# Hybrid encoder trunk on one core: layer norm issued in two stages, the split of w_out spread over the attention, convolution taps and pacing shifted, and the first two chunks multiplied side by side

## Chip, core and metric

The kernel runs on one core of a Trainium2 chip. A run's time is the device time of that core in microseconds (us), and a time given for a kernel is the median over its runs. PE (TensorE) multiplies, DVE (VectorE), ACT (ScalarE) and POOL (GpSimd) do the elementwise work, and SP issues the transfers.

## What is computed

One encoder layer on two batches with shared weights, a prompt of 512 rows and a sample of 1024, model width 1024:

```python
h = _rmsnorm(x, norm_attn_g[l])
z = h @ w_in[l]                       # q, k, v, ca, cb
a_out = _window_attn(q, k, v, bias, band, attn_sink[l])
c = ca * jax.nn.sigmoid(cb)
c = _dwconv(c, conv_dw_w[l], conv_dw_b[l])          # 31 taps per channel
c = jax.nn.silu(_layernorm(c, conv_ln_g[l], conv_ln_b[l]))
x = x + jnp.concatenate([a_out, c], axis=-1) @ w_out[l]
h = _rmsnorm(x, norm_ffn_g[l])
u = _dwconv(h @ w_up[l], ffn_dw_w[l], ffn_dw_b[l])  # 3 taps
x = x + (jax.nn.silu(u[..., :D_FF]) * u[..., D_FF:]) @ w_down[l]
return _rmsnorm(x, norm_final_g)
```

## The kernel before, in words

All is float32. Each operand is split into a high part and the rest (hi, lo), and a product is three matmuls (hi hi, hi lo, lo hi): L296, L297 and L299 for the projections by w_in and w_up, L711 to L713 for the one by w_out. A weight chunk is 128 output columns of 8 blocks of 128 rows, so 24 matmuls. `split` makes hi with an ACT cast (L189) and lo with a POOL subtraction (L190).

The stages in order: RMS norm of the prompt's four row blocks and their transposes (L255, evacuated as hi by ACT L257 and lo by DVE L258); 14 chunks of w_in for the prompt and 14 for the two halves of the sample, each result evacuated on DVE (L369 and others); the prompt's out-projection; the prompt's up-projection, 22 chunks of two halves (evacuated by ACT L841 and DVE L837, with a three-tap convolution); the sample's out-projection; then a feed-forward part for the sample, and the final norm.

Beside these matmul loops go side items. `tick`, called between matmuls, lets each queue go on at a rate: `pace` holds them (RA, RB, RBO, RD, RN, RE for attention and norms; CA, CB, CL, CLO, CD for the convolution). The items are:

- the depthwise convolution of a channel block (`conv_items`): of 31 taps the last NOFF are offloaded, multiplied on ACT (L331) and added on POOL (L332); the others accumulate on DVE in a PSUM bank (L335 first, L339 after it);
- attention, in units: score matmuls (L560), sink column copies (L537) and exponents with row sums on DVE (L567), probability scaling (L589, L595), transposes (L616), value matmuls (L630, L631) and their evacuation by ACT L638 and L639, DVE L640 and POOL L642. Units 0 to 7 are the prompt's, 8 to 23 the sample's, two to a block of 128 rows;
- `conv_norm(i)`, layer norm and silu of block i: load from DRAM, four transposes (L675), mean and variance on DVE (L677, L678), the power on POOL (L173, L174), normalising on DVE (L681), a wait of YN = 2 steps, four transposes back (L687), ACT L690 to L694 and DVE L693 and L695. Blocks 0 to 3 are the prompt's;
- in the sample's attention, behind its last unit, loading and splitting w_out in 21 pieces of which each step does one.

A PSUM bank is one of eight, tags a (3), u (2), b (2) and c (1); `use` says which tags a job may take, and a job whose bank is not evacuated waits. Up to the sample's out-projection the program order so paced goes through a scheduler that interleaves the instructions of each engine; behind it the order is written out by hand. Each engine works through its own list in order, so an instruction that waits holds up all behind it.

Of the kernel before, what the change touches and what calls it, by code (L numbers as in the profile page):

```python
# [39 lines left out]
RA, RB, RBO, RD, RN, RE = 1.2, 0.8, 2.5, 0.8, 0.95, 0.9  # L40
# [3 lines left out]
CL, CLO, CD = 0.6, 1.0, 0.6  # L44

NOFF = (4, 7)
# [6 lines left out]
YN = 2  # L53
OB = "uc"
VG = 3
NW = 36
KEEP = 3
# [85 lines left out]
def tile_hybrid_encoder(ctx: ExitStack, tc: tile.TileContext, xs, rel_bias, norm_attn_g, w_in,  # L143
# [28 lines left out]
    def rstd_of(ss, n, out):  # L172
        nc.gpsimd.tensor_scalar(out, ss, 1.0 / n, EPS, op0=ALU.mult, op1=ALU.add)  # L173
        nc.gpsimd.tensor_tensor(out, out, nhalf[:], op=ALU.pow)  # L174
# [26 lines left out]
    raws, ws = {}, {}  # L201

    def want_raw(i):
        if i < nch and i not in raws and i not in ws:
            raws[i] = chunk_raw(w_in[0], order[i][2])

    def want_w(i):
        if i < nch and i not in ws:
# [28 lines left out]

    def norm_in_place(x, k):
# [8 lines left out]
        nc.vector.tensor_scalar_mul(x[:], x[:], rs[:])  # L247

    marks = []

    def transposed(xn, g, h):
        for kc in range(KC):
# [8 lines left out]
            marks.append((ia.ins, iv.ins))  # L261
# [30 lines left out]
    def proj(out, w, h, late_lo=False):  # L292
        whi, wlo = w
        for kc in range(KC):
# [3 lines left out]
            if not late_lo:  # L298
                nc.tensor.matmul(out, wlo[:, kc, :], hi[:], start=False, stop=(kc == KC - 1))  # L299
            if kc % 2 == 1 and kc < KC - 1:  # L300
                tick()
        for kc in range(KC if late_lo else 0):
            nc.tensor.matmul(out, wlo[:, kc, :], h[kc][0][:], start=False, stop=(kc == KC - 1))
# [11 lines left out]
    def conv_items(g, c, cp):  # L315
# [3 lines left out]
        noff = NOFF[g]  # L319
# [97 lines left out]
    def make_h1(nt):  # L417
        xt = xq.pop(nt)
        for k, x in enumerate(xt):
            if nt == 1:  # L420
                with tc.issue_after(marks[KC - 1][0]), tc.issue_after(marks[KC - 1][1]):
                    norm_in_place(x, k)
# [7 lines left out]
    def step(i, nt):  # L430
        kind, c, col = order[i]
        pp = bank("step")
        proj(pp[:], ws[i], h1[nt], i < 2 and nt == 0)
# [13 lines left out]
    with tc.issue_after(marks[KC - 1][0]):  # L447
        want_w(1)
# [39 lines left out]
    for i in range(npr):  # L488
# [5 lines left out]
        if i == 1:  # L494
            constants()
            bbd = bias_to_dram()
        want_raw(i + 2)
        want_w(i + 1)
        step(i, 0)
        ws.pop(i)  # L500
# [161 lines left out]

    def conv_norm(i):
        G, b = blocks[i]
        if G["g"] == 0:
            drain(convs)
        cat = cat_of(i, 1)
# [14 lines left out]
        del pt  # L682
        for _ in range(YN):
            yield 0.0
# [84 lines left out]

    def prompt():  # L770
        yield from attention(0, 8, {u: conv_norm(u - 4) for u in range(4, 8)})
# [128 lines left out]
    def sample():  # L900
        sink_columns()
        yield from attention(8, 24)
# [740 lines left out]
```

## Time and profile before

| quantity | value |
|---|---|
| median of three runs | 1564.2 us (1560.03 to 1566.33) |
| profiled execution | 1558.91 us, of which the span is 1557.1 |
| busy share of the span | PE 97%, DVE 72%, ACT 51%, POOL 46% |
| HBM | 164.74 MB read, 62.14 MB written, 146 GB/s over the span |

The first matmul of a projection starts at 17 us, the prompt's out-projection at 278, its up-projection at 376 (first lo product), the last up-projection ends at 682, the sample's out-projection follows to about 790. A timeline row has the start, the length, the engine, the line, the operation with out<-in, and in brackets the idle time before it with what ended it. A row of waits has what PE stood for, with the sum, the number of times and the longest.

### The profile page before, as it was taken

What the parts mean: (1) busy time and instruction counts of PE and PEld (TensorE: products, weight loads), DVE (VectorE), ACT (ScalarE), POOL (GpSimd) and SP (SyncE); (2) the same over time, 40 slices, a digit from 0 to 9 for tenths busy, and PEclk for the clock granted to TensorE, in tenths of its full rate; (3) what the DMA queues carried; (4) which work ended last, traced back from release to release, by engine and by line L of the source; (5) the groups of instructions that cost most, each with busy time, mean ns of one, the idle gap of its engine ahead of it and who ended that gap; (6) DMA issues with size and microseconds to landing.
All of it is one profiled execution on the core that took longest, in us unless ns stands there. A gap on an engine that the chain in (4) does not pass through costs nothing. (4 is left out here: it accounts for less than half of the span.)

```text
span 1557.1 us, 20112 instructions
## 1 busy us (share of the span) xinstructions
PE 1506.9 (97%) x6843; PEld 1229.4 (79%) x6843; DVE 1126.2 (72%) x1604; ACT 795.4 (51%) x1404; POOL 708.9 (46%) x566
## 2 busy tenths in 40 slices
PE   8899998999999999899999999999999999999997
PEld 6787787787888888777777888888888788888885
DVE  7999767857788785344868777777776845568883
ACT  4634654335787786633454444455545543444254
POOL 7652344226666776947433455555554000003355
PEclk9999999999999999999999999999999999999999
DMA  7582334447343346779332233333331582356644
GB/s 230 156 212 81 107 100 124 129 142 217 112 132 129 118 129 181 242 238 298 114 93 76 92 104 104 105 104 102 102 115 64 200 284 82 105 165 230 221 135 162
DMA packets 228780, 227.17 MB, mean 146 GB/s; under 512 B 13268, under 2 KB 168348, under 8 KB 228549
## 3 DMA queue, kind: packets, MB, share of 16 engines
q1 hardware_dynamic: 228677, 225.88, 45.8%
q8 instruction: 54, 0.88, 0.2%
q14 instruction: 49, 0.40, 0.1%
HBM read 164.74 MB, written 62.14 MB: 146 GB/s over the span
## 5 line engine op out<-in xcount | busy, mean ns | idle before, releaser
L190 POOL TENSOR_TENSOR q<-q,q 128x1024 fp32r<-128x1024 f32 x72 | 173.4, 2415 | 93.4 <-ACT q L189 34.4
L940 POOL TENSOR_TENSOR q<-q,q 128x512 fp32r<-128x512 f32 x101 | 140.0, 1391 | 164.0 <-ACT q L1050 151.7
L940 DVE TENSOR_TENSOR h<-h,h 128x512 fp32r<-128x512 f32 (+2 forms) x202 | 153.9, 794 | 65.2 <-ACT h L944 25.3
L1398 PE MATMUL w<-h,h 128*128 128x512 f32 x462 | 181.4, 393 | 1.4 <-DVE q L1185 1.4
L1399 PE MATMUL w<-h,h 128*128 128x512 f32 x462 | 181.5, 393 | 0.0
L1400 PE MATMUL w<-h,h 128*128 128x512 f32 x462 | 181.1, 392 | 0.0
L1064 PE MATMUL w<-h,q 128*128 128x512 f32 x448 | 176.5, 394 | 1.0 <-ACT h L1147 0.6
L1066 PE MATMUL w<-h,q 128*128 128x512 f32 x448 | 175.5, 392 | 1.0 <-POOL q L940 1.0
L1065 PE MATMUL w<-h,q 128*128 128x512 f32 x426 | 166.4, 391 | 0.0
L296 PE MATMUL u<-h,q 128*128 128x512 f32 x400 | 161.0, 403 | 5.4 <-DVE h L837 4.1
L297 PE MATMUL u<-h,q 128*128 128x512 f32 x400 | 158.6, 397 | 0.0
L299 PE MATMUL u<-h,q 128*128 128x512 f32 x384 | 151.8, 395 | 2.7 <-POOL q L190 2.7
L937 POOL TENSOR_TENSOR q<-q,q 128x1024 f32<-128x1024 f32 x12 | 32.4, 2707 | 236.6 <-DVE q L937 220.0
L339 DVE SCALAR_TENSOR_TENSOR c<-c,cvw,c 128x512 f32<-128x512 f32 x184 | 138.0, 750 | 2.9
L944 ACT CAST h<-h 128x512 fp32r<-128x512 f32 x120 | 71.9, 619 | 93.2 <-DVE h L940 41.9
L296 PE MATMUL b<-h,q 128*128 128x512 f32 x256 | 102.7, 401 | 3.3 <-DVE d L369 2.2
L1398 PEld LDWEIGHTS w<-h,h 128*128 128x128 f32 x462 | 86.8, 188 | 21.6 <-ACT h L944 1.8
L1400 PEld LDWEIGHTS w<-h,h 128*128 128x128 f32 x462 | 86.7, 188 | 19.7
L1399 PEld LDWEIGHTS w<-h,h 128*128 128x128 f32 x462 | 86.8, 188 | 19.5
L837 DVE SCALAR_TENSOR_TENSOR h<-u,fw,h 128x511 f32<-128x511 f32 x88 | 65.5, 744 | 49.8 <-ACT h L841 49.0
L299 PE MATMUL b<-h,q 128*128 128x512 f32 x256 | 101.4, 396 | 0.0
L297 PE MATMUL b<-h,q 128*128 128x512 f32 x256 | 101.1, 395 | 0.0
(417 smaller groups left out, 3670.4 us busy)
## 6 DMA issues: line engine op xcount, KB each, us to landing
q<-in_w_up SPq DMA_DIRECT2D x88, 512.0 KB
ga<-q SPq DMA_DIRECT2D x64, 256.0 KB
h<-ga SPq DMA_DIRECT2D x57, 256.0 KB
q<-in_w_in SPq DMA_DIRECT2D x28, 512.0 KB
h<-in_w_down SPq DMA_DIRECT2D x52, 256.0 KB
q<-in_x_sample SPq DMA_DIRECT2D x15, 512.0 KB
h<-qsd SPq DMA_DIRECT2D x24, 256.0 KB
x1d<-q SPq DMA_DIRECT2D x11, 512.0 KB
```

The costliest lines, as they stand in the source:

```text
L190: (nc.vector if dve else nc.gpsimd).tensor_tensor(lo[:], raw[:], hi[:].bitcast(F32), op=ALU.subtract)
L296: nc.tensor.matmul(out, whi[:, kc, :], hi[:], start=(kc == 0), stop=False)
L297: nc.tensor.matmul(out, whi[:, kc, :], lo[:], start=False, stop=False)
L299: nc.tensor.matmul(out, wlo[:, kc, :], hi[:], start=False, stop=(kc == KC - 1))
L339: nc.vector.scalar_tensor_tensor(acc[:], src(t), w(t), acc[:], op0=ALU.mult, op1=ALU.add)
L940: (eng or nc.vector).tensor_tensor(out, a, b, op=ALU.subtract)
L1064: nc.tensor.matmul(out, whi[:, s], hi[:], start=(start and c == 0), stop=False, **go)
L1065: nc.tensor.matmul(out, whi[:, s], lo[:], start=False, stop=False, **go)
L1066: nc.tensor.matmul(out, wlo[:, s], hi[:], start=False, stop=(stop and c == 3), **go)
L1398: nc.tensor.matmul(out, sh[:, c], th[:], start=(p == 0), stop=False)
L1399: nc.tensor.matmul(out, sh[:, c], tl[:], start=False, stop=False)
L1400: nc.tensor.matmul(out, sl[:, c], th[:], start=False, stop=(p == NPAIR - 1))
```

## The change

1. `conv_norm` is cut in two generators. `conv_norm_1` loads, transposes, and normalises; `conv_norm_2` transposes back and finishes. For the prompt, stage 1 of block u-3 comes behind unit u and stage 2 of it behind unit u+1, with stage 1 of the next; for the sample, stage 1 of blocks 4 and 5 comes first, and then stage 2 of one and stage 1 of the one two on.
2. The 21 pieces of w_out for the sample start behind unit WOU = 19, two at each unit, and what is left comes behind unit 23.
3. NOFF goes from 4 (prompt) and 7 (sample) to 7 for every prompt channel block, and 10, 10, 7, 7 for the sample's.
4. Rates: RD 0.8 to 0.84, RN 0.95 to 0.9, CL 0.6 to 0.45, CLO 1.0 to 0.8, CD 0.6 to 0.62.
5. `first_two` multiplies chunks 0 and 1 beside each other, block by block, in two banks. Their casts come ahead of the prompt's hi parts on ACT, and the transposes there may also take bank c. `late_lo` and the step order of these two chunks are dropped.
6. The RMS norm's odd row blocks take mean and epsilon in the DVE reduction, without POOL's multiply-add; the final norm takes the mean in ACT's square and has one POOL instruction fewer in `finish`.

```diff
-RA, RB, RBO, RD, RN, RE = 1.2, 0.8, 2.5, 0.8, 0.95, 0.9
+RA, RB, RBO, RD, RN, RE = 1.2, 0.8, 2.5, 0.84, 0.9, 0.9
-CL, CLO, CD = 0.6, 1.0, 0.6
-NOFF = (4, 7)
+CL, CLO, CD = 0.45, 0.8, 0.62
+NOFF = ((7, 7, 7, 7), (10, 10, 7, 7))
-YN = 2
+WOU = 19
...
     def norm_in_place(x, k):
...
-            nc.vector.tensor_tensor_reduce(out=junk[:], in0=x[:], in1=x[:], scale=1.0, scalar=0.0,
+            nc.vector.tensor_tensor_reduce(out=junk[:], in0=x[:], in1=x[:], scale=1.0 / D, scalar=EPS,
                                            op0=ALU.mult, op1=ALU.add, accum_out=ss[:])
-        rstd_of(ss[:], D, rs[:])
+        if k % 2 == 0:
+            root = rstd_of(ss[:], D, rs[:])
+        else:
+            root = nc.gpsimd.tensor_tensor(rs[:], ss[:], nhalf[:], op=ALU.pow)
...
-        noff = NOFF[g]
+        noff = NOFF[g][c]
...
+    def first_two():
+        pp = [bank("step") for _ in range(2)]
+        for kc in range(KC):
+            hi, lo = h1[0][kc]
+            for i in range(2):
+                whi = ws[i][0]
+                nc.tensor.matmul(pp[i][:], whi[:, kc, :], hi[:], start=(kc == 0), stop=False)
+                nc.tensor.matmul(pp[i][:], whi[:, kc, :], lo[:], start=False, stop=False)
+            if kc % 2 == 1:
+                tick()
+        for i in range(2):
+            for kc in range(KC):
+                nc.tensor.matmul(pp[i][:], ws[i][1][:, kc, :], h1[0][kc][0][:], start=False, stop=(kc == KC - 1))
+            kind, c, _ = order[i]
+            evac(kind, c, 0, pp[i][:])
...
-    for _ in make_h1(0):
+    use.update(turn="aubc")
+    for k, x in enumerate(xq[0]):
+        norm_in_place(x, k)
+    his = []
+    for i in range(2):
+        hi = sb.tile([KC, P], F32R)
+        nc.scalar.copy(hi[:], raws[i][:])
+        his.append(hi)
+    h1[0] = []
+    for _ in transposed(xq.pop(0), gA, h1[0]):
         pass
-    with tc.issue_after(marks[0][0]):
-        want_w(0)
+    use.update(turn="aub")
+    with tc.issue_after(marks[3]):
+        for i in range(2):
+            lo = sb.tile([KC, P], F32R)
+            nc.gpsimd.tensor_tensor(lo[:], raws.pop(i)[:], his[i][:].bitcast(F32), op=ALU.subtract)
+            ws[i] = his[i], lo
...
         nc.vector.tensor_scalar(xh[:], pt[:], mv[:, 0:1], rs[:], op0=ALU.subtract, op1=ALU.mult)
-        del pt
-        for _ in range(YN):
-            yield 0.0
+        normed[i] = xh
+        yield 0.0
+
+    def conv_norm_2(i):
+
+        cat, xh = cat_of(i, 1), normed.pop(i)
         p2 = bank("norm")
...
-        yield from attention(0, 8, {u: conv_norm(u - 4) for u in range(4, 8)})
+        yield from attention(0, 8, {u: both(*([conv_norm_2(u - 4)] if u > 3 else []), *([conv_norm_1(u - 3)] if u < 7 else []))
+                                    for u in range(3, 8)})
...
+        wos = wo_pieces()
+        yield from attention(8, 24, {u: some(wos, 2) for u in range(WOU, 24)})
         kt.clear(), vt.clear(), qt.clear(), bias.clear(), score_rows.clear()
         use.update(norm="a")
         pace.update(rate=RN)
+        yield from wos
         drain(late)
+        yield from conv_norm_1(4)
+        yield from conv_norm_1(5)
         for m in range(NE):
-            yield from conv_norm(4 + m)
+            yield from conv_norm_2(4 + m)
+            if NE + 4 + m < NB:
+                yield from conv_norm_1(4 + NE + m)
...
-            nc.scalar.activation(o[:, s], parts[n], AF.Square, accum_out=ss[:, n:n + 1])
-        nc.gpsimd.tensor_scalar(rs[:, 0:1], ss[:, 0:1], 1.0 / D, EPS, op0=ALU.mult, op1=ALU.add)
-        nc.gpsimd.tensor_scalar(rs[:, 1:2], ss[:, 1:2], 1.0 / D, rs[:, 0:1], op0=ALU.mult, op1=ALU.add)
+            nc.scalar.activation(o[:, s], parts[n], AF.Square, scale=D ** -0.5, accum_out=ss[:, n:n + 1])
+        nc.gpsimd.tensor_scalar(rs[:, 1:2], ss[:, 1:2], ss[:, 0:1], EPS, op0=ALU.add, op1=ALU.add)
```

How the order changes is shown at three places. Lines in the changed kernel have moved: L303 to L305 are the projection (L296, L297, L299 before), L600 the scores (L560), L607 the exponents (L567), L577 the sink copies (L537), L891 and L895 the up evacuation on DVE and ACT (L837, L841), L721 and L736 the norm's two transposes (L675, L687), L760 to L762 the out-projection (L711 to L713), L670 and L671 the values (L630, L631).

First, PE at the end of the prompt's attention, where the norm of the last blocks stands; before:

```order
L299 MATMUL b_149_2641<-h_105_649,q_383_2500 128x512
L675 MATMUL a_142_2510<-ident,q_370_2386 128x128 [waits DMAHW4_49,Activation_49]
L675 MATMUL a_142_2510<-ident,q_370_2386 128x128 x3
L687 MATMUL u_144_2540<-ident,q_387_2522 128x128 [waits DVE_49]
L687 MATMUL u_144_2540<-ident,q_387_2522 128x128 x3
L675 MATMUL a_150_2668<-ident,h_400_2660 128x128 [waits DMAHW6_49,PE_49]
L675 MATMUL a_150_2668<-ident,h_400_2660 128x128 x3
L687 MATMUL u_152_2701<-ident,h_404_2680 128x128 [waits DVE_49,Activation_49]
L687 MATMUL u_152_2701<-ident,h_404_2680 128x128 x3
L630 MATMUL a_148_2602<-h_391_2584,h_162_954 128x512 [waits Activation_49]
L711 MATMUL u_154_2812<-h_418_2765,h_216_1309 128x512 [waits Activation_49]
```

and now, where b_147, b_151 and b_153 are banks of w_in chunks for the sample:

```order
L303 MATMUL b_147_2618<-h_128_742,q_384_2405 128x512 [waits DVE_49]
L721 MATMUL a_145_2573<-ident,h_402_2564 128x128 [waits DMAHW5_49]
L721 MATMUL a_145_2573<-ident,h_402_2564 128x128 x3
L304 MATMUL b_147_2618<-h_129_743,q_384_2405 128x512
...
L304 MATMUL b_151_2696<-h_109_654,q_400_2553 128x512
L736 MATMUL u_150_2675<-ident,h_406_2585 128x128 [waits DVE_49]
L736 MATMUL u_150_2675<-ident,h_406_2585 128x128 x3
L305 MATMUL b_151_2696<-h_108_653,q_401_2554 128x512
L303 MATMUL b_153_2793<-h_128_742,q_400_2553 128x512 [waits DVE_49]
...
L305 MATMUL b_153_2793<-h_152_868,q_401_2554 128x512
L760 MATMUL u_152_2786<-h_429_2743,h_225_1329 128x512 [waits DVE_49,Activation_49]
```

Before, the first and second transposes of two blocks stood directly behind each other; now 54 rows of projections and attention stand between the two of the last block, and 25 matmuls behind them ahead of the out-projection.

Second, PE at the second block of the sample's attention, beside the prompt's up chunks (u_); before:

```order
L299 MATMUL u_180_3613<-h_503_3355,q_532_3557 128x512
L560 MATMUL b_187_3757<-q_507_3406,h_557_3732 128x256 [waits DVE_49]
L560 MATMUL b_187_3757<-q_508_3407,h_557_3732 128x256
L560 MATMUL a_192_3813<-q_509_3412,h_558_3734 128x256 [waits DMAHW6_49,DMAHW7_49,DMAHW2_49,DVE_49]
L560 MATMUL a_192_3813<-q_510_3413,h_558_3734 128x256 [waits DMAHW5_49]
L296 MATMUL u_181_3656<-h_487_3265,q_537_3601 128x512 [waits DVE_49,Activation_49]
L297 MATMUL u_181_3656<-h_488_3266,q_537_3601 128x512
```

and now four score pairs in a row, ahead of the next up chunk:

```order
L305 MATMUL u_181_3692<-h_516_3335,q_559_3638 128x512
L600 MATMUL b_187_3799<-q_528_3442,h_579_3771 128x256 [waits DVE_49]
L600 MATMUL b_187_3799<-q_529_3443,h_579_3771 128x256
L600 MATMUL a_192_3858<-q_530_3448,h_580_3773 128x256 [waits DVE_49]
L600 MATMUL a_192_3858<-q_531_3449,h_580_3773 128x256
L600 MATMUL a_199_3978<-q_528_3442,h_588_3823 128x384 [waits DMAHW6_49,DVE_49]
L600 MATMUL a_199_3978<-q_529_3443,h_588_3823 128x384
L600 MATMUL a_200_3982<-q_528_3442,h_588_3823 128x384 [waits DVE_49]
...
L303 MATMUL u_183_3745<-h_499_3241,q_565_3688 128x512 [waits DVE_49,Activation_49]
L304 MATMUL u_183_3745<-h_500_3242,q_565_3688 128x512
```

with this on DVE, where a_186, a_191, a_192 and b_187 are the score banks that the exponents release:

```order
L607 ISA q_576_3762,s_581_3775<-a_186_3795,h_543_3542,nsink 128x256 [waits DMAHW2_49]
...
L607 ISA q_576_3762,s_581_3775<-b_187_3799,h_544_3544,nsink 128x256 [waits DMAHW5_49,PE_49]
...
L891 SCALAR_TENSOR_TENSOR h_564_3684<-u_180_3649,fw,h_564_3684 128x511 [waits Activation_49]
L343 SCALAR_TENSOR_TENSOR c_194_3908<-c_472_3008,cvw,c_194_3908 128x512 [waits DVE_49]
L891 SCALAR_TENSOR_TENSOR h_569_3727<-u_181_3692,fw,h_569_3727 128x511 [waits Activation_49]
L577 COPY q_578_3768<-nsink 128x1 [waits DMAHW3_49,Pool_49]
...
L607 ISA q_578_3768,s_589_3825<-a_191_3854,h_547_3550,nsink 128x256 [waits DMAHW7_49]
...
L607 ISA q_578_3768,s_589_3825<-a_192_3858,h_548_3552,nsink 128x256 [waits DMAHW4_49,PE_49]
L607 ISA s_589_3825 128x1
L629 RECIPROCAL s_582_3776<-s_582_3776 128x4 [waits Activation_49]
L891 SCALAR_TENSOR_TENSOR h_564_3684<-u_180_3649,fw,h_564_3684 128x511 [waits DVE_49]
```

The exponents of b_187, a_191 and a_192 stand with three up evacuations and a convolution tap among them, and the score pair of a_199 takes the bank that a_191 held.

Third, PE at the last block of the sample's attention, where c_377 is a bank of the sample's out-projection, b_360 holds the last values and u_365 is an up chunk:

```order
L305 MATMUL u_363_6519<-h_516_3335,c_1038_6457 128x512
L761 MATMUL c_377_6839<-h_1030_6416,h_992_6234 128x512 [waits Pool_49]
L762 MATMUL c_377_6839<-h_1029_6415,h_993_6235 128x512
L670 MATMUL b_360_6449<-h_1031_6430,h_535_3459 128x512 [waits Activation_49]
L671 MATMUL b_360_6449<-d_1032_6431,h_535_3459 128x512 [waits DVE_49]
L670 MATMUL b_360_6449<-d_1033_6445,h_535_3459 128x512
L671 MATMUL b_360_6449<-q_1034_6446,h_535_3459 128x512
L303 MATMUL u_365_6582<-h_499_3241,q_1047_6515 128x512 [waits DVE_49,Activation_49]
L304 MATMUL u_365_6582<-h_500_3242,q_1047_6515 128x512
L305 MATMUL u_365_6582<-h_499_3241,q_1048_6516 128x512 [waits Pool_49]
```

with this on ACT, where L678 and L679 evacuate the values and q_1047 is the hi part of the chunk for u_365:

```order
L895 ACTIVATE h_1059_6564<-u_363_6519,vecs,fw 128x512 [waits PE_49]
L915 ACTIVATE b_361_6460<-h_1020_6382 128x512 [waits DVE_49]
L678 COPY h_1041_6491<-b_360_6449 64x512 [waits DVE_49,PE_49]
L679 CAST h_1006_6308<-b_360_6449 64x512
L189 CAST q_1047_6515<-q_1036_6454 128x1024 [waits DMAHW2_49,Pool_49]
L189 CAST h_1044_6507<-h_989_6222 128x512 [waits DMAHW1_49,DVE_49]
L895 ACTIVATE h_1046_6511<-u_362_6468,vecs,fw 128x512 [waits Pool_49]
```

The cast of the chunk and the up evacuation of u_362 (L895) stand behind the evacuation of the values, with a cast of a w_out piece (h_1044) between.

More of the change, by code (lines that the diff above doesn't have):

```diff
@@ L200, in tile_hybrid_encoder @@
     nch = len(order)
-    raws, ws = {}, {}
+    raws, ws, asked = {}, {}, set()
     def want_raw(i):
-        if i < nch and i not in raws and i not in ws:
+        if i < nch and i not in raws and i not in ws and i not in asked:
+            asked.add(i)
             raws[i] = chunk_raw(w_in[0], order[i][2])
     def want_w(i):
-        if i < nch and i not in ws:
+        if 1 < i < nch and i not in ws:
             want_raw(i)
@@ L290, in drain, with proj @@
             advance(queue)
-    def proj(out, w, h, late_lo=False):
+    def proj(out, w, h):
         whi, wlo = w
@@ L899, in tile_hybrid_encoder, with wo_pieces @@
     load_bias()
[L900 to L905 removed]
+    def wo_pieces():
         for m in range(16 + WOA):
```

57 lines of the change are left out of this document (38 added, 19 removed).

## Prediction

> **What bounds the kernel now.** I read the page first, then the waits of PE (TensorE), then the windows around the longest of them.
>
> ```profile
> span 1557.1 us, 20112 instructions
> PE 1506.9 (97%) x6843; PEld 1229.4 (79%) x6843; DVE 1126.2 (72%) x1604; ACT 795.4 (51%) x1404; POOL 708.9 (46%) x566
> ```
>
> ```profile
> PE u L296 <- DVE h L837: 4.1, 2, 3.5
> PE u L687 <- DVE q L681: 4.0, 1, 4.0
> PE u L687 <- DVE h L681: 2.9, 1, 2.9
> PE u L299 <- POOL q L190: 2.7, 2, 1.5
> PE u L711 <- DVE s L678: 2.2, 1, 2.2
> PE b L296 <- DVE d L369: 2.2, 1, 2.2
> PE u L616 <- DVE s L567: 2.0, 2, 1.1
> PE a L560 <- DVE s L567: 1.7, 1, 1.7
> PE a L675 <- DMA h<-cvd: 1.4, 1, 1.4
> PE a L687 <- DVE h L681: 0.7, 1, 0.7
> ```
>
> ```profile
> 270.00:280.00 10.00, 5.37 (x18) 4.37 (x19) 5.05 (x8) 6.67 (x15) 5.36 (x8) 0.50 0.47 152
> 280.00:290.00 10.00, 10.00 (x44) 7.89 (x44) 7.15 (x11) 5.77 (x11) 1.75 (x2) 1.00 0.74 217
> 650.00:660.00 10.00, 5.91 (x19) 4.14 (x18) 4.30 (x6) 3.23 (x6) 9.92 (x7) 0.83 0.72 215
> 680.00:690.00 10.00, 7.81 (x34) 6.22 (x33) 6.00 (x9) 4.70 (x9) 6.06 (x9) 0.83 1.05 370
> ```
>
> PE is the bound: busy 1506.9 of 1557.1 us, so 50.2 us is all that better order can win, besides the time at half clock. No arithmetic is saved on PE; the change can pay only in PE's waits, and the ten rows above (columns: sum, times, longest) are 23.9 us of them. The window rows (stretch, length, busy time of PE, its weight loads, DVE, ACT, POOL, granted clock, DMA share, GB/s) show the second price of a wait. The clock was 0.50 all through 270 to 280, where PE was busy 5.37 us: at full clock half of that, 2.7 us, would do. In 650 to 660 and 680 to 690 the 0.83 means 3.4 us at half clock (10 x 0.17 / 0.5), in which 1.7 us of work is lost.
>
> **The change part by part** (all against the profiled execution).
>
> *Start, -0.8.* Two chunks of w_in are cast ahead of the first hi of the transposed activations.
>
> ```profile
> 14.02 0.69 ACT L257 ACTIVATE h<-u,vecs 128x512 fp32r<-128x512 f32 x1 [5.23 <-PE u L255]
> 14.61 1.03 ACT L189 CAST q<-q 128x1024 fp32r<-128x1024 f32 x1
> 17.07 0.70 PE L296 MATMUL u<-h,q 128*128 128x512 f32 x1 [0.87 <-DVE h L258]
> ```
>
> ACT was idle 5.23 us ahead of 14.02, room for two casts of 1.03; the second hi then need not stand behind one (up to 1.03 sooner), and the first matmul follows its lo. Against that, it now needs two banks empty where one did: I take -0.8, between -1.5 and 0. The missing POOL multiply-add of the odd tiles I cost at nothing: the multiplications by rstd on DVE are in a row behind each other either way.
>
> *The bank behind the convolution, -2.2.*
>
> ```profile
> 50.39 0.75 DVE L247 TENSOR_SCALAR q<-q,s 128x1024 f32<-128x1024 f32 x1 [0.44 <-POOL s L174]
> 51.72 0.68 DVE L369 SCALAR_TENSOR_TENSOR d<-h,b 128x512 f32<-128x512 f32 x1
> 52.45 0.50 PE L296 MATMUL b<-h,q 128*128 128x512 f32 x1 [2.19 <-DVE d L369]
> ```
>
> A bank's evacuation (L369) waited on DVE behind the second batch's normalise (L247). In the new order ten taps stand ahead of it and nothing of the second batch's normalise: the 2.2 go; if the ten taps are late instead, they come back with up to 2.
>
> *Taps from DVE to ACT and POOL, 0 in the sum.* Per tap and half row ACT multiplies and POOL adds where DVE multiplied and added:
>
> ```profile
> L339 DVE SCALAR_TENSOR_TENSOR c<-c,cvw,c 128x512 f32<-128x512 f32 x184 | 138.0, 750 | 2.9
> L331 ACT ACTIVATE h<-c,cvw 128x512 f32<-128x512 f32 x38 | 26.8, 720 | 13.9 <-PE u L712 5.3 <-PE a L631 2.2 <-DMA qsd<-h 1.6
> L332 POOL TENSOR_TENSOR h<-h,h 128x512 f32<-128x512 f32 x47 | 62.2, 1322 | 61.1 <-ACT h L331 60.0
> ```
>
> Prompt: 4 channels x 3 taps = 12. Sample: 2 channels x 3 taps x 2 halves = 12. DVE loses 24 x 0.75 = 18.0 us, ACT gains 17.3, POOL 24 x 1.32 = 31.7. DVE stays under 72%, POOL rises from 46 to 48%; beside PE's 97% this is hidden, except where POOL is full (next parts). In the prompt's attention the waits of L616 and L560 (3.7 us) lie behind DVE's queue; part of them goes, but the second stage of the norms, now between the blocks, puts others there (a score bank read behind L677 and L681). I set this at 0, between -3 and +3.
>
> *Layer norm in two stages, -9.5.*
>
> ```profile
> 271.69 1.12 PE L687 MATMUL u<-ident,q 128*128 128x128 f32 x4 [4.03 <-DVE q L681]
> 276.61 1.09 PE L687 MATMUL u<-ident,h 128*128 128x128 f32 x4 [2.94 <-DVE h L681]
> ```
>
> Two blocks' transposes, L675 and L687, came directly behind each other, and both trips through DVE and POOL lay bare: 4.03 + 2.94 = 7.0 us, and 2.7 of half clock. In the new order 50 matmuls of 512 columns stand between the two transposes of the last block and 25 the second, ahead of the first out-projection. At 0.23 us each (44 in the 10 us from 280 on) the 50 are 11 us of cover for a trip of 4. 9.7 go; I leave 0.2. If the late stage were itself behind a full queue, the bound is the old 4.0, thus -9.7 to -5.7.
>
> *Start of the up-projection, +2.4.* POOL makes the lo half of every up chunk.
>
> ```profile
> 366.70 6.78 POOL L332 TENSOR_TENSOR h<-h,h 128x512 f32<-128x512 f32 x5
> 375.87 0.50 PE L299 MATMUL u<-h,q 128*128 128x512 f32 x1 [1.48 <-POOL q L190]
> ```
>
> Five adds in a row held POOL 6.78 us there, and PE waited 1.48 for the split behind them. With ten instead of seven taps on POOL for the first two sample channels, two or three adds more stand ahead of the early splits: 3 x 1.32 = 4.0, of which I expose 2.4 (half way, 0 to 5).
>
> *First scores of the sample's attention, +5.7.* Four pairs of score matmuls stand in a row now (before: two, then an up chunk). The third pair's bank is released by a DVE exponent that is queued behind up-projection evacuations. Durations as spaced on DVE in the same stage before:
>
> ```profile
> 384.13 0.21 DVE L537 COPY q<-nsink 128x1 f32<-128x1 f32 x2
> 387.04 0.48 DVE L567 CUSTOM_DVE_ANT_0 q<-a,h,nsink 128x256 f32<-128x256 f32 x1
> 387.45 0.48 DVE L567 CUSTOM_DVE_ANT_0 q<-b,h,nsink 128x256 f32<-128x256 f32 x1
> 388.51 0.74 DVE L837 SCALAR_TENSOR_TENSOR h<-u,fw,h 128x511 f32<-128x511 f32 x1
> 389.17 0.75 DVE L339 SCALAR_TENSOR_TENSOR c<-c,cvw,c 128x512 f32<-128x512 f32 x1
> ```
>
> From the last up matmul: copies 0.13, two exponents 0.41 each, evacuation, tap, evacuation 0.66 each, copies 0.13, exponent 0.41 make 3.5; another exponent, a reciprocal and an evacuation 1.25: 4.7, with some 0.4 for handing over 5.1, less PE's own 1.2 of score matmuls: 4.0 of waits. At 1.7 for half clock (as in 680 to 690) 5.7. Low end 0, if the DVE work runs ahead; high end 8.
>
> *Last attention block, +0.9.*
>
> ```profile
> 651.70 0.62 ACT L189 CAST h<-h 128x512 fp32r<-128x512 f32 x1 [1.32 <-DMA h<-in_w_out]
> 653.26 0.77 ACT L841 ACTIVATE h<-u,vecs,fw 128x512 f32<-128x512 f32 x1
> 654.07 1.53 DVE L837 SCALAR_TENSOR_TENSOR h<-u,fw,h 128x511 f32<-128x511 f32 x2 [0.52 <-ACT h L841]
> 655.75 0.76 PE L296 MATMUL u<-h,q 128*128 128x512 f32 x1 [3.45 <-DVE h L837]
> L189 ACT CAST q<-q 128x1024 fp32r<-128x1024 f32 x72 | 75.4, 1050 | 49.1 <-DMA q<-in_w_in 20.8 <-POOL q L190 11.1 <-DMA q<-in_w_up 9.1
> L638 ACT COPY h<-b 64x512 f32<-64x512 f32 x7 | 4.1, 580 | 1.1 <-PE b L631 1.1
> ```
>
> Here an ACT cast that waited 1.32 for its piece of w_out held up the evacuation behind it. With the pieces asked for earlier that wait goes, but the order now puts the last block's tail in the same place: four matmuls, then ACT 0.58 + 0.58 + 1.05 + 0.62 + 0.77 = 3.6 and two DVE steps 1.5, then the next up chunk. 5.0 for the old 4.1: +0.9 (-4 if ACT is ahead, +3). One smaller trip of this kind stands some 300 rows earlier (three exponents in turn ahead of transposes): +1.2, taken under the 1.7 of L560's longest.
>
> *Sample out-projection, -5.6.* Ten out matmuls (10 x 0.23) now stand where PE waited 2.2 for the last up bank (L711), and with it went 1.7 of half clock (680 to 690): -3.5 of 3.9. The waits of L675 and L687 (1.4 + 0.7) go because the next block's first stage is issued a step ahead: -2.1. *Final norm, -0.3:* one POOL instruction fewer behind the last matmul.
>
> Sum: -0.8 - 2.2 - 9.5 + 2.4 + 5.7 + 0.9 + 1.2 - 5.6 - 0.3 = -8.2. The profiled execution took 1558.9, 5.3 under the median of the three runs, 1564.2; so I forecast 1564.2 - 8.2 = 1556.0.
>
> **Rivals.** *The new waits stay hidden.* For it: two score pairs that stood together in this stage of before are not among the longest waits. Then 5.7, 2.4, 0.9 and 1.2 fall away: -18.4, 1545.8. Against it: the chains are read from instructions that wait for each other by name, and the same reading gives 4.0 for the old norm.
>
> *The clock stays full at the first scores.* Its longest single wait would be about 2.5 us. Without the 1.7: -9.9, 1554.3. The Trainium skill (TensorE: Matmul & The Clock Gate, "What's actually happening") has the clock halve only after an idle window of about 3.4 us, which would give this case. The window 680 to 690 speaks against it: 2.2 us of waiting was followed by 3.4 us at half clock.
>
> *POOL becomes the bound, slower.* POOL was busy 9.92 of 10 us in 650 to 660. If it is full from the sample's convolution up to the out-projection, its 12 additional adds for the sample, 12 x 1.32 = 15.8, reach PE through the lo halves; the forecast's own 2.4 is part of that: -8.2 + 13.4 = +5.2, and with two more half-clock stretches (3.4) +8.6: 1572.8. It decides from the point where POOL shows no idle time before the split that PE waits for; POOL's 46% over the span speaks against it.
>
> *The stages do not come apart.* If the tail of the norm still lies bare (5.7 gained, not 9.5), -4.4: 1559.8.
>
> **How the numbers follow.** Two measurements of this kernel can be told apart from about 0.5%, 7.8 us: faster is under 1556.4, slower over 1572.0. Chances: forecast 0.50, waits hidden 0.22, clock full 0.08, POOL 0.12, stages not apart 0.08. The forecast lies on the border, so half of it counts as faster; with the hidden waits and most of the clock case that is 0.53; slower is the POOL case, 0.12; the rest, 0.35, is no change. The range takes in the forecast's bounds and the hidden waits: 1543 to 1569; the slower rival and the far end below are left out. The likeliest case's own range is 1550 to 1563.
>
> **What would show it.** Right: no wait of the norm's second transposes over 1 us and a clock of 1.00 in the 10 us before the prompt's out-projection; first matmul near 16.3; new PE waits of together 4 us at the first sample scores, released by DVE's exponent and the up evacuation; still 3 to 5 us at the last attention block. Wrong: those places show no wait (then about 1546), or PE waits for POOL's lo halves in several chunks (then over 1570).

## The result and the profile after

The changed kernel takes 1590.6 us (median of 4 runs, 1589.7 to 1592.5) against 1562.9 before (now four runs): ratio 1.0177, 95% interval 1.0156 to 1.0198. I had forecast 1556.0 and at most 1569. The profiled execution has a span of 1588.0 us, 30.9 more than before.

The page of the changed kernel:

```profile
span 1588.0 us, 20184 instructions
PE 1519.0 (96%) x6843; PEld 1236.1 (78%) x6843; DVE 1126.9 (71%) x1580; ACT 809.4 (51%) x1428; POOL 741.8 (47%) x572
```

The same matmuls are 12.1 us longer busy and PE is idle 18.8 us more (69.0 against 50.2). The longer busy time is mostly clock: over the span the granted clock is 0.983 for 0.990, and the windows below have means of 0.51 to 0.83. The rows of PE's waits (sum, times, longest) that are used below:

```profile
PE u L303 <- DVE h L891: 8.9, 2, 8.7
PE u L670 <- ACT h L658: 5.1, 1, 5.1
PE u L305 <- POOL q L190: 3.7, 2, 2.0
PE a L600 <- DVE s L607: 3.2, 2, 2.4
PE u L303 <- ACT q L189: 2.5, 3, 1.4
PE u L760 <- ACT h L189: 1.9, 1, 1.9
PE u L600 <- DVE q L680: 1.8, 1, 1.8
```

No row of the norm's second transposes (L736) is there, and none of L760 waiting for the sample's last up bank: what the change set out to take away is gone. In its place stand an up chunk that waits 8.7 us for an evacuation (L303, at the last attention block), values that wait for ACT (L670, at 240 us), and waits for the hi and lo halves of weights (L189, L190). Windows around them, in the columns of the prediction:

```profile
240.00:250.00 10.00, 7.49 (x24) 5.46 (x25) 4.87 (x11) 7.01 (x17) 2.41 (x4) 0.67 0.38 92
375.00:385.00 10.00, 7.59 (x26) 5.66 (x27) 5.89 (x9) 4.00 (x6) 9.92 (x7) 0.83 0.33 100
409.00:419.00 10.00, 9.77 (x37) 7.70 (x38) 9.82 (x22) 5.58 (x14) 2.23 (x2) 0.83 0.08 28
680.00:690.00 10.00, 3.80 (x9) 3.04 (x10) 2.89 (x4) 4.40 (x7) 6.10 (x4) 0.51 0.58 202
```

The largest, followed back (rows picked out): ACT first, then DVE, then PE.

```profile
683.06 0.62 ACT L189 CAST h<-h 128x512 fp32r<-128x512 f32 x1 [2.74 <-DMA catd<-h]
683.70 0.78 ACT L895 ACTIVATE h<-u,vecs,fw 128x512 f32<-128x512 f32 x1
684.51 1.54 DVE L891 SCALAR_TENSOR_TENSOR h<-u,fw,h 128x511 f32<-128x511 f32 x2 [4.57 <-ACT h L895]
686.20 0.76 PE L303 MATMUL u<-h,q 128*128 128x512 f32 x1 [8.71 <-DVE h L891]
```

The chain is the one that I had read from the order, cast of a w_out piece and all. What I had not priced is the bracket of its first row: the cast waited 2.74 us for a store. Its output goes to a buffer whose content was still on its way to catd, and ACT's queue stood behind it. At 240 us a cast on ACT had waited for a load some 7 us earlier:

```profile
233.43 1.05 ACT L189 CAST q<-q 128x1024 fp32r<-128x1024 f32 x1 [3.42 <-DMA q<-in_w_in]
240.18 0.79 PE L670 MATMUL u<-h,h 128*128 128x512 f32 x1 [5.10 <-ACT h L658]
```

And at the end of the program, where 15.9 us lie between PE's last matmul and the end of the span (10.7 before), a square waits for a store to have left its buffer:

```profile
1578.97 0.63 ACT L1516 ACTIVATE q<-q 128x512 f32<-128x512 f32 x1 [3.32 <-DMA out_sample<-q]
```

In all three places ACT waits for a transfer, and at two of them for a store to leave a buffer. Whether buffers are short shows, for the whole program, in what SP waits for before it issues a weight load (L183); before, and after:

```profile
SPq L183 <- PE u L299: 55.9, 19, 6.2
SPq L183 <- PE u L297: 55.4, 15, 7.2
SPq L183 <- POOL q L190: 19.1, 2, 15.2
```

```profile
SPq L183 <- POOL q L190: 120.4, 34, 8.1
SPq L183 <- PE u L305: 19.3, 4, 5.7
```

Before, a load went into a buffer that PE's last matmul on an old chunk had set free. After, 34 loads wait for POOL to read the raw weights of a chunk just split: the ring of large buffers (15 of 4 KB, tag q) has become shorter by one. The cause is in the diff. The start of the changed kernel loops over the four prompt tiles in the outer function, `for k, x in enumerate(xq[0])`, where the loop was in a generator before. A buffer goes back when the last reference to its tile falls, and x, never set again in the outer function, holds the fourth tile to the end of the program. How much of each wait above is this buffer's only the runs can tell (e9).

### The profile page after: what moved, and what is told of

Same layout as the page of the kernel before. It is cut to its first block, busy times and chain, and to the rows that moved or that the text cites. A ratio compares the mean times of both kernels' runs of the same rounds, so it can differ in the third digit from the quotient of the medians.

```text
span 1588.0 us, 20184 instructions
## 1 busy us (share of the span) xinstructions
PE 1519.0 (96%) x6843; PEld 1236.1 (78%) x6843; DVE 1126.9 (71%) x1580; ACT 809.4 (51%) x1428; POOL 741.8 (47%) x572
## 5 line engine op out<-in xcount | busy, mean ns | idle before, releaser
L190 POOL TENSOR_TENSOR q<-q,q 128x1024 fp32r<-128x1024 f32 x69 | 165.9, 2405 | 103.9 <-ACT q L189 84.1
L1008 POOL TENSOR_TENSOR q<-q,q 128x512 fp32r<-128x512 f32 x81 | 113.6, 1414 | 150.3 <-ACT q L1118 147.2
L303 PE MATMUL u<-h,q 128*128 128x512 f32 x376 | 152.5, 406 | 11.3 <-DVE h L891 8.9
L305 PE MATMUL u<-h,q 128*128 128x512 f32 x376 | 150.5, 401 | 3.7 <-POOL q L190 3.7
L304 PE MATMUL u<-h,q 128*128 128x512 f32 x376 | 150.4, 400 | 0.0
L1132 PE MATMUL w<-h,q 128*128 128x512 f32 x368 | 146.3, 398 | 2.7 <-ACT h L1215 2.3
L1134 PE MATMUL w<-h,q 128*128 128x512 f32 x368 | 144.7, 393 | 0.6 <-POOL q L1008 0.6
L1005 POOL TENSOR_TENSOR q<-q,q 128x1024 f32<-128x1024 f32 x9 | 24.0, 2671 | 250.8 <-DMA h<-gb 198.4
L1133 PE MATMUL w<-h,q 128*128 128x512 f32 x346 | 136.7, 395 | 0.0
L343 DVE SCALAR_TENSOR_TENSOR c<-c,cvw,c 128x512 f32<-128x512 f32 x172 | 129.1, 751 | 2.3
L303 PE MATMUL b<-h,q 128*128 128x512 f32 x256 | 103.2, 403 | 1.9 <-ACT h L364 0.7
L336 POOL TENSOR_TENSOR h<-h,h 128x512 f32<-128x512 f32 x65 | 84.8, 1305 | 42.0 <-ACT h L335 40.0
L305 PE MATMUL b<-h,q 128*128 128x512 f32 x256 | 101.4, 396 | 0.0
```

What stands on the lines that cost most here:

```text
L190: (nc.vector if dve else nc.gpsimd).tensor_tensor(lo[:], raw[:], hi[:].bitcast(F32), op=ALU.subtract)
L303: nc.tensor.matmul(out, whi[:, kc, :], hi[:], start=(kc == 0), stop=False)
L304: nc.tensor.matmul(out, whi[:, kc, :], lo[:], start=False, stop=False)
L343: nc.vector.scalar_tensor_tensor(acc[:], src(t), w(t), acc[:], op0=ALU.mult, op1=ALU.add)
L1008: (eng or nc.vector).tensor_tensor(out, a, b, op=ALU.subtract)
L1132: nc.tensor.matmul(out, whi[:, s], hi[:], start=(start and c == 0), stop=False, **go)
```

## The experiments

Theory S, at first: the early pieces of w_out hold buffers, and casts wait behind stores. Rival N: the new taps and rates load POOL and ACT. Rival O: every new order draws new waits of this size. Theory L, the lost buffer, came with e9. Ratios are to the kernel before on the same chip, with 95% intervals.

**e1, w_out late in the changed kernel.**

```diff
-WOU = 19
+WOU = 24
```

> The changed kernel with the 21 pieces of w_out again behind the last attention unit (WOU = 24), all else kept. Theory S (buffers still being stored): the pieces, loaded early, hold buffers through the last attention blocks, so casts get buffers whose stores to catd have not gone out, and the wait of 8.7 us at the last block with its 10 us of half clock comes from that; then this run is 12 to 16 us faster than the changed kernel, about 1576. Rival N (the numbers: taps and rates load POOL and ACT): the wait stays, time within 4 us of 1590.6. Rival O (every new order draws new waits of this size): the wait goes but others of 5 us or more come at new places, and the time is anywhere from 1565 to 1590.

1583.1 us, ratio 1.0121 (1.0101 to 1.0142): 7.5 faster than the changed kernel, half of what S asked for. The 8.7 us wait went, others stayed (4.6 at 242, 3.3 at 293), and so did 15.7 us behind PE's end. S explains a part.

**e2, the old taps and rates in the changed kernel.**

```diff
-RA, RB, RBO, RD, RN, RE = 1.2, 0.8, 2.5, 0.84, 0.9, 0.9
+RA, RB, RBO, RD, RN, RE = 1.2, 0.8, 2.5, 0.8, 0.95, 0.9
-CL, CLO, CD = 0.45, 0.8, 0.62
-NOFF = ((7, 7, 7, 7), (10, 10, 7, 7))
+CL, CLO, CD = 0.6, 1.0, 0.6
+NOFF = ((4, 4, 4, 4), (7, 7, 7, 7))
```

> The changed kernel with the taps (4 and 7) and the five rates of before; two-stage norm, spread of w_out, start and final norm kept. Theory S: the last block keeps a wait of 5 us or more, and the time stays above 1580. Rival N: the waits at 240, 375 to 412, and 686 go with the load on POOL and ACT, and the time falls by 15 us or more, to 1575 or below. Rival O: the list of waits is a new one, with no place in common but the start and the final norm.

1581.6, ratio 1.0113 (1.0093 to 1.0133): 9 faster. Neither S (above 1580, but with 3.4 us at the last block, not 5) nor N (1575).

**e3, the two-stage norm alone on the kernel before.** The cutting of `conv_norm` in two and the calls in the sample, as in the change, belong to it and are not shown again.

```diff
...
-        yield from attention(0, 8, {u: conv_norm(u - 4) for u in range(4, 8)})
+        yield from attention(0, 8, {u: both(*([conv_norm_2(u - 4)] if u > 3 else []), *([conv_norm_1(u - 3)] if u < 7 else []))
+                                    for u in range(3, 8)})
...
-            side.appendleft(conv_norm(i + NE))
+            side.appendleft(both(conv_norm_2(i + NE), *([conv_norm_1(i + NE + 2)] if i + NE + 2 < NB else [])))
```

> The kernel before with the layer norm in two stages and nothing else. My prediction's terms: norm -9.5 and the sample's norm -2.1, so 1551 to 1553 for a median of before near 1563. Theory S says the same, since nothing here holds more buffers. Rival O: the 7 us of norm waits go but 5 us or more come at new places, and the time is 1555 to 1575.

1584.2, ratio 1.0127 (1.0107 to 1.0147): 21 us slower, outside what any of the theories gave. The norm's 7 us are gone, and one wait of 10.1 stands a little later:

```profile
PE u L720 <- ACT h L189: 10.1, 1, 10.1
```

It is the first out-projection of the prompt (L720 there), for the cast of its w_out piece, and on ACT ahead of that cast stands one of a w_in chunk whose load came late:

```profile
303.70 1.04 ACT L189 CAST q<-q 128x1024 fp32r<-128x1024 f32 x1 [4.56 <-DMA q<-in_w_in]
304.65 0.61 ACT L189 CAST h<-h 128x512 fp32r<-128x512 f32 x1
```

**e4, a hundredth on one rate of the kernel before.**

```diff
-RA, RB, RBO, RD, RN, RE = 1.2, 0.8, 2.5, 0.8, 0.95, 0.9
+RA, RB, RBO, RD, RN, RE = 1.2, 0.8, 2.5, 0.81, 0.95, 0.9
```

> The kernel before with one rate moved by a hundredth (RD 0.80 to 0.81): no work added or taken, only the points at which side items are issued. Theory S and rival N: nothing that they speak of changes, within 3 us of before. Rival O: the order of the up-projection stage is dealt anew, and the time moves by 5 us or more in either direction (more likely up, as the order of before is one with few waits).

1571.0, ratio 1.0048 (1.0032 to 1.0064): 7.5 us for nothing but another order. This is what O says, and it is a measure of what one order is worth.

**e5, the final norm alone.**

```diff
-            nc.scalar.activation(o[:, s], parts[n], AF.Square, accum_out=ss[:, n:n + 1])
-        nc.gpsimd.tensor_scalar(rs[:, 0:1], ss[:, 0:1], 1.0 / D, EPS, op0=ALU.mult, op1=ALU.add)
-        nc.gpsimd.tensor_scalar(rs[:, 1:2], ss[:, 1:2], 1.0 / D, rs[:, 0:1], op0=ALU.mult, op1=ALU.add)
+            nc.scalar.activation(o[:, s], parts[n], AF.Square, scale=D ** -0.5, accum_out=ss[:, n:n + 1])
+        nc.gpsimd.tensor_scalar(rs[:, 1:2], ss[:, 1:2], ss[:, 0:1], EPS, op0=ALU.add, op1=ALU.add)
```

> The kernel before with the final norm's edit alone (mean in ACT's square, one POOL instruction fewer for each block). PE's order stays as it is up to the last part. My prediction's term: -0.3, and the stretch from PE's end to the end of the span 10.4 us (10.7 before, 15.9 in the changed kernel). Rival: the edit itself makes the end longer (ACT waits for the store of a buffer), then 15 to 16 us there and +5 in all. If it stays at 10 to 11, the 5 us of the changed kernel's end come with other buffers, not with this edit.

1562.9, ratio 0.9996 (0.9977 to 1.0015): no effect on the time that can be told. Behind PE's end lie 12.9 us, between the two expectations; that this edit is not the source of the longer end is shown by e9 and e11 below, which have it and end in 10.4 and 10.6.

**e6, start and final norm alone.** Cut out of the changed kernel: with the rates of e2 also, and with the norm in one stage for the sample too:

```diff
-NOFF = ((7, 7, 7, 7), (10, 10, 7, 7))
+NOFF = ((4, 4, 4, 4), (7, 7, 7, 7))
-WOU = 19
+WOU = 24
...
+        yield from attention(0, 8, {u: conv_norm(u - 4) for u in range(4, 8)})
```

> The kernel before with the start (two chunks side by side, casts ahead, RMS norm without POOL's multiply-add) and the final norm; taps, rates, norm in one stage and w_out as before. My prediction's terms: -0.8 - 0.3, so 1 us under before. Rival O (a new order draws new waits): first matmul about 0.8 earlier, but 5 to 20 us more waits elsewhere, between 120 and 790 us above all, 1568 to 1583. End: if 15 us or more follow PE's end here, the start's buffers carry through to the end.

1570.1, ratio 1.0045 (1.0025 to 1.0064), with 17.0 us behind PE's end, 4 more than with the final norm alone. So the start, 1550 us earlier, seems to lengthen the end. That sent me to what the start keeps.

**e7, the taps alone on the kernel before.**

```diff
-NOFF = (4, 7)
+NOFF = ((7, 7, 7, 7), (10, 10, 7, 7))
-        noff = NOFF[g]
+        noff = NOFF[g][c]
```

> The kernel before with the taps alone (7 for the prompt; 10, 10, 7, 7 for the sample). My prediction: 0 in the sum, with +2.4 at the start of the up-projection, so 1563 to 1566. Rival N: POOL is late for the lo halves in several chunks between 370 and 680 us, +8 to +12 there. Rival O: +5 to +20, with waits that are not POOL's.

1567.4, ratio 1.0016 (0.9999 to 1.0034): little, though 1.4 us over what I expected. The largest new wait is ACT's, not POOL's (5.0 us at 368.6, L296 for L257), which speaks for O and against N.

**e8, a hundredth on one rate of the changed kernel.**

```diff
-RA, RB, RBO, RD, RN, RE = 1.2, 0.8, 2.5, 0.84, 0.9, 0.9
+RA, RB, RBO, RD, RN, RE = 1.2, 0.8, 2.5, 0.83, 0.9, 0.9
```

> The changed kernel with one rate moved by a hundredth (RD 0.84 to 0.83), nothing else. Rival O: the waits between 375 and 810 are dealt anew and the time moves by 4 to 12 us, and as the changed kernel's order is not a lucky one, down as easily as up: 1578 to 1598. If the waits are set by the work itself (theory S or N), within 3 us of 1590.6.

1593.7, ratio 1.0187 (1.0137 to 1.0236): 3 us, not the 4 to 12 of O. One other order does not bring the changed kernel back, which speaks for something other than bad luck.

**e9, the buffer given back.**

```diff
     his.clear()
-    hi = lo = None
+    x = hi = lo = None
```

> The changed kernel with one name set to None after the start. The start's loop over the four prompt tiles now stands in the outer function, and its loop variable x keeps the fourth tile, one of the 15 large buffers, to the end of the program; setting x to None gives the buffer back. No instruction is added or taken. Theory L (the lost buffer): loads of weights wait for buffers and casts for stores, so the waits at 240, 290, 375 to 412 and 686 shrink, the stretch behind PE's end falls from 15.9 to about 10.7, and the time falls by 20 us or more, to 1570 or below, perhaps to the 1556 that I forecast. Rival O (only the new order): the end may fall by 5 us, the rest is dealt anew: 1578 to 1592.

1562.0, ratio 0.9994 (0.9980 to 1.0008): one name costs 28.6 us, more than the change as a whole. Behind PE's end 10.4 us are left, no square waits over 2 us for out_sample, and SP's loads wait for PE again:

```profile
SPq L183 <- PE u L304: 63.3, 16, 7.7
SPq L183 <- PE u L305: 47.3, 15, 5.3
SPq L183 <- POOL q L190: 21.8, 4, 13.8
```

The waits that I had named in the expectation did not all shrink. At 400 to 410, where the first scores now stand, PE waits for nothing and the clock is full. But PE still waits 3.7 at 236 and 3.1 at 288, and at the last attention block the same cast still waits for a store, 1.00 for 2.74, and PE 7.2 for 8.7:

```profile
400.00:410.00 10.00, 10.00 (x49) 8.46 (x48) 9.21 (x21) 5.75 (x15) 5.25 (x4) 1.00 0.26 81
666.49 0.62 ACT L189 CAST h<-h 128x512 fp32r<-128x512 f32 x1 [1.00 <-DMA catd<-h]
669.62 0.76 PE L303 MATMUL u<-h,q 128*128 128x512 f32 x1 [7.22 <-DVE h L891]
```

So the largest wait of the changed kernel is for the greater part not the buffer's. Between the two profiled executions (22.6 us apart; that of e9 was its slowest of ten) 10.5 us lie from the first to the last matmul of the prompt's up-projection, 5.5 behind PE's end, and the rest in small parts.

**e10, one large buffer less in the kernel before.**

```diff
-    sb = Slots(big, dict(q=(15, 4096), c=(4, 4224), h=(61, 2048), d=(2, 2176), s=(32, 64)), "q", KEEP)
+    sb = Slots(big, dict(q=(14, 4096), c=(4, 4224), h=(61, 2048), d=(2, 2176), s=(32, 64)), "q", KEEP)
```

> The kernel before with 14 large buffers in place of 15 from the start on, nothing else changed. Theory L: slower by 10 to 25 us, the stretch behind PE's end 15 to 17 us, and two of the pieces of w_out in halves of large buffers. Rival O: within 8 us of before, as for any small change of order, and the end stays at 10 to 13.

1577.4, ratio 1.0097 (1.0078 to 1.0115): 13.8 us, with 16.7 behind PE's end and the same mark on SP; only the guess on w_out's pieces was wrong (all 32 in small buffers).

```profile
SPq L183 <- POOL q L190: 106.3, 35, 7.7
```

e9 and e10 show the cause from both sides. All twenty kernels, those of the runs below included, agree on the mark: in the six with a large buffer less (the changed one, e1, e2, e6, e8, e10) 31 to 36 loads wait for POOL, 104 to 136 us in all, and 15.7 to 17.7 us lie behind PE's end; in the fourteen others it is 2 to 7 loads, 2 to 37 us, and 9.3 to 12.9. Among the fourteen are e3, e15 and e16, which lose 20 to 60 us by other orders or other buffers and do not bear it.

What the buffer costs depends on the kernel around it: 28.6 in the changed one (e9), 25.8 with RD at 0.83 (e8 against e12), 23.3 with w_out late (e1 against e13), 13.8 in the kernel before (e10) and 6.0 with the start and final norm alone (e6 against e11). The early w_out is thus some 5 us of it at most. Since giving a buffer back also deals the later ones anew, each of these figures may hold some of that too.

**e11, start and final norm with the buffer given back:** e6, and

```diff
-    hi = lo = None
+    x = hi = lo = None
```

> The start and the final norm alone, with the buffer given back. Theory L: the 7 us that start and final norm cost alone go, 6 of them behind PE's end (17.0 to about 10.7), 1562 to 1564. Rival O: the end stays at 15 to 17, 1568 to 1573.

1564.1, ratio 1.0007 (0.9994 to 1.0020): the 6 us of e6 are the buffer's, 10.6 behind PE's end.

**e12, buffer back and RD 0.83:** the edits of e8 and e9 together.

> The changed kernel with the buffer given back and RD at 0.83 in place of 0.84, to see how far the time with the buffer back hangs on one order. Theory L: within 6 us of the run with the buffer given back alone. Rival O: 8 us or more apart from it.

1567.9, ratio 1.0032 (1.0016 to 1.0048): 5.8 slower than e9, within L's 6.

**e13, buffer back and w_out late:** e9, and

```diff
-WOU = 19
+WOU = 24
```

> The changed kernel with the buffer given back and the pieces of w_out again behind the last attention unit. Open: where the 8.2 us that I forecast went, since with the buffer back the change gives nothing. If the spread of w_out eats them (wait of 7.2 and 5 us of half clock at the last attention block), this run is 5 to 9 us faster than 1562.0, and no wait over 4 us stands between 600 and 700. If not, within 3 us of it.

1559.8, ratio 0.9972 (0.9958 to 0.9986): faster than the kernel before, by little. The wait at the last attention block falls from 7.2 (e9) to 2.3:

```profile
PE u L303 <- DVE h L891: 7.2, 1, 7.2
```

```profile
PE u L303 <- DVE h L891: 3.9, 3, 2.3
PE u L760 <- ACT h L189: 3.5, 1, 3.5
```

So the early w_out costs some 2 us of time, less than its wait; the intervals of e9 and e13 overlap, so even this is not certain.

**e14, buffer back and the norm in one stage:** e9, and

```diff
         yield from conv_norm_1(i)
+        yield 0.0
         yield from conv_norm_2(i)
...
+        yield from attention(0, 8, {u: conv_norm(u - 4) for u in range(4, 8)})
```

> The changed kernel with the buffer given back and the layer norm in one stage, its two transposes kept at least a step apart. If the two-stage norm gives what I forecast for it (9.5 and 2.1), this run is 8 to 12 us slower, 1570 to 1574, with waits of 7 us at the second transposes near 275. If what it takes away comes back as other waits before the prompt's out-projection (235 to 290 with the buffer back: 3.7, 1.8 and 3.2), within 4 us of 1562.

1571.2, ratio 1.0045 (1.0028 to 1.0062): 9.2 slower than e9, the size that I had forecast for the two stages. But its waits are not the 7 us at the second transposes; the largest is 8.1 at the last attention block, and the norm's transposes wait for a load:

```profile
PE u L303 <- DVE h L891: 8.4, 2, 8.1
PE u L722 <- DMA h<-cvd: 3.6, 2, 2.2
```

The size came out, the mechanism did not.

**e15 and e16, one small buffer more**, on e9 and on the kernel before.

```diff
-    sb = Slots(big, dict(q=(15, 4096), c=(4, 4224), h=(61, 2048), d=(2, 2176), s=(32, 64)), "q", KEEP)
+    sb = Slots(big, dict(q=(15, 4096), c=(4, 4224), h=(62, 2048), d=(2, 2176), s=(32, 64)), "q", KEEP)
```

> The changed kernel with the buffer given back and 62 instead of 61 small buffers (2 KB each). Theory L in the other direction: if buffers still limit the loads and the casts, no piece of w_out has to go to half a large buffer any more, the waits at 235 to 290 and at the last block get shorter, and the time falls by 3 to 8 us. If the 8.2 went to waits that are not about buffers, within 3 us, or moved by a new order by up to 8 either way.

> The kernel before with 62 small buffers. If buffers limit it too, 2 to 6 us faster; if not, within 3 us, or up to 8 slower by a new order.

1618.1, ratio 1.0332 (1.0295 to 1.0369), and 1624.1, ratio 1.0385 (1.0363 to 1.0407). Neither expectation: over 50 us slower. Most of it (40 of 67 us between the profiled executions of e16 and before) is in the hand-ordered feed-forward part, which waits at regular steps where this wait came to 0.3 us before (e16):

```profile
PE w L1064 <- ACT w L1138: 23.8, 8, 3.4
```

What is given out next depends on what is free, so another count deals all later buffers anew; why this deal costs so much I did not follow further. As a test of whether buffers still limit these kernels the two runs say nothing.

**e17, buffer back, structure only:** e9 with the edits of e1 and e2, so start, two stages and final norm are left. **e18, two stages with the new taps and rates:** the kernel before with the edits of e3 and e7 and the five rates of the change.

> The changed kernel with the buffer given back, and with the taps, the rates and the late w_out of before: start, two-stage norm and final norm are left. If taps and rates cost what they cost alone (e7, +4.5), this run is 3 to 6 us faster than e13 (1559.8), about 1555. If the two-stage norm needs the new taps and rates to pay (alone it cost 21 us, e3, in the changed kernel it gave 9), it is slower than e13 by 5 us or more.

> The kernel before with the two-stage norm, the new taps and the new rates; start, w_out and final norm as before. If the numbers were chosen for the two-stage norm, the wait of 10 us ahead of the prompt's out-projection in e3 goes and the time is 1560 to 1566. If the start makes the difference, the wait stays and the time is above 1575.

1564.3, ratio 1.0004 (0.9986 to 1.0023), and 1564.2, ratio 1.0004 (0.9988 to 1.0021). e18 came out as its first expectation, e17 half a microsecond short of its second. The 21 us of e3 go with either companion, so they belong to one order, not to the two stages. Against e11, which has the norm in one stage, e17 gains nothing.

## Why the prediction was wrong

**The step that failed** is the very first of the change part by part, and no term stands for it: the start. I worked out two casts moved ahead, -0.8, and took the rest of those lines as a rewriting of the same loop. That x now outlives its loop costs 28.6 us (e9). The order of instructions that I read has it in no row, since no instruction is added; it shows only in which buffer each instruction writes. The sum priced every DMA wait in the new order at nothing, though the order rows in the section on the change mark them: the h_1044 cast at the last block "waits DMAHW1_49", and that was the store (2.74 us, and 1.00 with the buffer back).

**Term by term**, in the changed kernel's trace:

- Start, -0.8: first matmul at 16.29 for 17.07. Right in this trace; with the same instructions at the start it came at 15.88 in e12 and at 17.32 in e9, so one trace does not settle a term of this size.
- Bank behind the convolution, -2.2: that wait went, and 1.8 and 1.5 stand at 60 and 62, with a half clock. From 50 to 70 PE is idle 4.0 us for 4.2 before, at a clock of 0.91 for 1.00: no gain.
- Taps, 0: e7 gives +0.2% with an interval that touches none. Right within what can be told.
- Norm, -9.5: the waits at L736 are gone, and 5.1, 1.8 and 1.9 stand at 240, 248 and 290 in the same stage. The gain was there and was given back before the stage ended. Whether the stages are worth 9.2 (e14), nothing (e17 against e11) or less than nothing (e3) depends on the order around them.
- Start of the up-projection, +2.4: 1.4, 1.7 and 2.1 of waits for L189 and L190 between 375 and 395, 5.1 for the 1.5 of before, 3.6 more where I had 2.4. With the buffer back no wait for a split in that stretch is over 0.6 (e9), so this is the lost buffer's; the adds expose nothing there.
- First scores, +5.7: 0.8 and 2.4 at 406 and 409, and 3.4 us at half clock (409 to 419: 0.83), 4.9. Right in place and nearly in size, and PE waits there for DVE's exponents, as I read it. But with the buffer back the wait is gone (e9; PE waits for nothing between 380 and 420 in e12 and e13 either): the chain does not lie bare by itself, and that the size came out was luck. The clock halved after a wait of 2.4 at the longest, so the rival that drew on the Trainium skill's idle window of 3.4 us (TensorE: Matmul & The Clock Gate, "What's actually happening") fell here too; the measurement decides.
- Last attention block, +0.9 on 4.1 (two waits, of which 3.5 at this place): 8.7. The round trip that I read is there, and its size was wrong: 7.2 with the buffer back, 2.3 with w_out late also (e13), so most of the excess goes with the early w_out in this order; with w_out early and RD at 0.83 the longest such wait is 2.4 (e12). Of the 2.74 us of waiting for a store 1.00 is left in e9. The 10 us at half clock cost little beyond the wait, for PE was busy in 3.80 us of 680 to 690.
- Sample out-projection, -5.6: all its waits over 1 us went. Right.
- Final norm, -0.3: the edit is worth nothing that can be told (e5); the end grew by 5.2, the lost buffer's (e11).

**The rivals.** POOL as the bound, at 0.12, gave 1572.8 and is wrong as a cause. The sign that I had named for it is there: ahead of the splits that PE waits for at 380 and 394 POOL goes from adds of the convolution straight into the split. But all of PE's waits for such splits are 3.7 us (L305), 0.2 of them are left with the buffer given back, and the taps alone cost 0.2% (e7). None of my cases held a loss of 28. That the new waits stay hidden, at 0.22, holds for the first scores and the splits once the buffer is back, and not for the last attention block; its 1545.8 did not come even so.

**And without the lost buffer?** The forecast of -8.2 would have been wrong still: e9 is at 0.9994, some -0.9. As the first scores (+5.7) and the splits (+2.4) cost nothing there, the rest of my sum is -16.3, and what has to be explained is 15 us rather than 7. Part of the answer may be e13 (early w_out, 2.3 us) and part e4: a hundredth on a rate costs 7.5 us. The one neighbour of the order of before that was run is slower, which fits an order that had been picked, but one neighbour does not show it. My sum took the waits I could name out of it and kept all others at their old size, but an edit deals all the others anew: e4, e12 and e8 move by 7.5, 5.8 and 3.0. How much of the missing 15 is that and how much each edit stays open; with differences of this size no single order tells.

## What to carry to other kernels

Where buffers go back when a name falls, a loop moved out of a function into the body around it can hold a buffer to the end: look in the diff for every name that outlives its loop, before counting instructions. In a trace such a loss has a mark of its own: the load queue waits for the engine that reads raw data where it waited for the engine that uses it, and the end of the program gets longer though nothing there was changed. And when a hundredth on a pacing number moves the time by half a per cent, sums of single waits cannot tell gains of that size; measure each edit on several orders.

## What the runs showed that I had not expected

One of 15 large buffers is worth 13.8 us to one kernel and 28.6 to the other (e10, e9). One small buffer more costs 56 us on e9 and 60 on the kernel before (e15, e16); that the buffers are then dealt out otherwise is the likely reason. The clock halves after less waiting than the largest wait suggests: 2.4 us with 0.8 shortly before it was enough at 409, and one wait of 8.7 brought 10 us of half clock, while the 2.2 us at 52 in the kernel before brought none (50 to 60: 1.00).
